# Decay-block copies moved to ScalarE, two multiplies to VectorE and two planner prices raised, in a two-layer decoder trunk

## The chip, the cores and the metric

The kernel runs on one core of one Trainium2 chip. The metric is device time in microseconds (us) for one execution; lower is better. The time of the kernel before is 627.79 us, the median of three runs (627.25, 627.79 and 630.24).

## What is computed

The input is 512 tokens of 1,024 numbers in fp32. Two layers follow one another, each added to its own input. Every multiplication with weights is done as three products of fp32r halves (high part by high part, low by high, high by low).

```python
for layer in range(DEPTH):                     # 2
    h = rms_norm(x, norm_w[layer])
    if layer % 2 == 0:                         # layer 0
        y = even_layer(h, ...)  # projection, mLSTM (4 heads) beside
                                # sparse attention (8 heads), projection
    else:                                      # layer 1
        y = hgrn2_layer(h, ...) # projection, HGRN2 (8 heads), projection
    x = x + y

# mLSTM branch, after its scan h:
h = rms_norm(h, head_norm)
return h * sigmoid(o) * silu(z)

# HGRN2: A holds q.k under the decay between two tokens of a chunk
A = einsum('bhjc,bhsc,bhjsc->bhjs', qj, kj, dec)
o = einsum('bhjs,bhsv->bhjv', A, vj) + einsum('bhjc,bhcv->bhjv', qj*exp(bcum), S)
```

## The kernel before, in words

**The order is planned, not written.** The program's strands call wrapped engines (`Paced`, L540, and `PacedPE`), which only record an operation with its dependencies and a price in nanoseconds from `price` (L516). At the end of each layer `flush` (L391) runs a list scheduler (`schedule`, L283) for 6 rounds, keeps the plan with the earliest end, and only then issues every instruction, from one line, L407. So nearly all rows of the profile have line L407 and are told apart by the names of their tiles, and a changed price redraws the order of all engines and of the DMA queue on SP. On an engine the instructions then run in the planned order.

**Dense products.** `cvt_w` (L736) turns a raw weight tile (`raw`, three buffers, loaded by SP) into a high half `whi` (two copies on ACT) and a low half `wlo` (a subtraction on DVE). The activations are split likewise: `h0h` and `h0l` in layer 0, `h1h` and `h1l` in layer 1, `ymh` and `yml` for layer 0's output projection. PE writes the products to PSUM tiles `mm`, `sc`, `ac`, `mx` and `my`; small products and transposes go to `tp`, `tq` and `sd`.

**Start.** The first products need `whi`, `wlo`, `h0h` and `h0l` for eight pieces of 128 input columns. Beside them ACT squares the input (`acc` and `sq`) for the norm. `rstd` (L892) sums these squares on PE, adds EPS on DVE, takes the power -0.5 on POOL (L900) and spreads the result by PE (`tq<-cs,rs` in layer 1).

**mLSTM tail.** `m_tok(t)` (L1485) divides, norms and gates one chunk of 128 tokens. Its array `nd` is multiplied by `hr` (L1515) and by the gate `gz` (L1517) on POOL, once more on DVE, transposed by PE and split into `ymh` and `yml`. POOL also issues the copies of weight tiles named `wt`.

**HGRN2.** `hgrn(h)` (L1771) builds for a head the array `f` (called `AT` there) of 128 x (4 x 128): its diagonal 32 x 32 blocks come out of `AL` (written by six predicated copies on DVE) by four copies on POOL (L1841 to L1843), each of 32 partitions by 4 x 32; the larger off-diagonal blocks come from `tq` by ACT. Then PE computes `tq<-ivgg,f` and `tq<-Sx,HB`, ACT squares (`hj`), POOL takes a power (`hr`). Transposed keys are evacuated by ACT as `kT`.

Of the kernel before, what the change touches and what calls it, by code (L numbers as in the profile page):

```python
# [16 lines left out]
AF = mybir.ActivationFunctionType  # L17
OP = mybir.AluOpType
# [128 lines left out]
def cust(ap, dims, off=0):  # L147
    return bass.AP(tensor=ap.tensor, offset=ap.offset + off,
                   ap=[list(ap.ap[0])] + [list(d) for d in dims])
# [278 lines left out]
class Mark:  # L428
    t = None
# [86 lines left out]
def price(name, fn, a, k):  # L516

    aps = [x for x in (*a, *k.values()) if isinstance(x, bass.AP)]
    n = max(free_size(x) for x in aps)
    psum = any(x.tensor.name[:3] in PSUMS for x in aps[1:])  # L520
    scal = sum(1 for x in aps[1:] if free_size(x) == 1 and n > 1)
    if name == "A":
        return (55 if psum else 93) + 95 * scal + (88 if "accum_out" in k else 0) + 0.833 * n - (95 if "accum_out" in k else 0)
    if name == "V":
        if fn in ("tensor_scalar", "tensor_copy") and not psum:
            return 67 + 61 * scal + 0.53 * n
        return 67 + 61 * scal + 1.045 * n
    if k.get("op") == OP.pow:
        return 300 + 165 * n
    if fn == "memset":  # L530
        return 32 + 0.86 * n
    if fn == "tensor_copy":
        return 547
    return 150 + (2.1 if fn == "tensor_tensor" else 0.86) * n
# [5 lines left out]
class Paced:  # L540
# [5 lines left out]
    def __getattr__(self, fn):  # L546
        f = getattr(self.eng, fn)

        def go(*a, **k):
            aps = [x for x in a if isinstance(x, bass.AP)]  # L550
            ns = price(self.name, fn, a, k)
            self.flow.work(self.name, ns)
            for x in aps:
                if x.tensor.name in self.flow.last:
                    self.flow.last[x.tensor.name] = self.flow.cur.t
            self.plan.add(self.name, f, a, k, ns)
        return go
# [56 lines left out]
def build(tc, I, out):  # L614
    nc = tc.nc
    fl, pl = Flow(), Plan()
    V, A, P = (Paced(fl, e, n, pl) for e, n in ((nc.vector, "V"), (nc.scalar, "A"), (nc.gpsimd, "P")))
# [3 lines left out]
    with ExitStack() as ctx:  # L621
# [42 lines left out]
        def cut(t, shape, p=slice(0, 128)):  # L664
            n = 1
            for d in shape:
                n *= d
            v = t[p, :n]
            if len(shape) == 1:
                return v  # L670
            ls = "abcdef"[:len(shape)]
            return v.rearrange("p (" + " ".join(ls) + ") -> p " + " ".join(ls), **dict(zip(ls, shape)))
# [32 lines left out]
        hm = cp.tile([128, 16], F32, name="hm")  # L705
# [186 lines left out]
        def rstd(accs, rs, rsB, ev, TPS=TPS, tp_t=tp_t):  # L892
            yield [None, TPS]
            p = tp_t()
            for i in range(NT):
                for a in accs:
                    T.matmul(p[:, i:i + 1], a[:, 128 * i:128 * (i + 1)], shc("one", 1), start=a is accs[0],
                             stop=a is accs[-1], skip_group_check=True)
            V.tensor_scalar(rs, p[:, :4], 1.0 / D, EPS, op0=OP.mult, op1=OP.add)
            P.tensor_tensor(rs, rs, hm[:, :4], op=OP.pow)  # L900
            fl.mark(ev[0]).op = pl.ops[-1]
            yield [None, TPS]
            p = tp_t()
            for i in range(NT):
                T.matmul(p[:, 128 * i:128 * (i + 1)], cust(rs, [[0, 128]], i), idf, start=True, stop=True,
                         skip_group_check=True)
            A.activation(rsB, p, AF.Copy)
            fl.mark(ev[1])
# [36 lines left out]
        with ExitStack() as c0:  # L945
# [45 lines left out]
            rs = rs0  # L991
# [493 lines left out]
            def m_tok(t):  # L1485
                sl = slice(128 * t, 128 * (t + 1))
                yield [E("mh%d" % h) for h in range(4)] + [hb(1)]
                nd = b_t("nd", (4, 129))
                for h in range(4):
                    yield SCS  # L1490
                    p = sc_t()
                    T.matmul(p[:, :129], Sm[0][:, h, sl], vx[0][:, t, h, :], start=True, stop=True,
                             skip_group_check=True)
                    if t:
                        T.matmul(p[:, 256:385], mqk["mq"][:, h, sl], Cx[0][:, t - 1, h, :], start=True, stop=True,
                                 skip_group_check=True)
                        A.activation(nd[:, h, :], p[:, 256:385], AF.Copy,
                                     scale=ex[:, 16 + 4 * t + h:16 + 4 * t + h + 1])
                        V.tensor_tensor(nd[:, h, :], nd[:, h, :], p[:, :129], op=OP.add)
                    else:  # L1500
                        A.activation(nd[:, h, :], p[:, :129], AF.Copy)
                dd = s_t("dd", [128, 4])
                V.scalar_tensor_tensor(dd, nd[:, :, 128], -1.0, nd[:, :, 128], op0=OP.mult, op1=OP.max)
                V.tensor_tensor(dd, dd, ex[:, 32 + 4 * t:36 + 4 * t], op=OP.max)
                rd = s_t("rd", [128, 4])
                V.reciprocal(rd, dd)
                hs = s_t("hs", [128, 4])
                hj = s_t("hj", [128, 128], 1)
                for h in range(4):
                    A.activation(hj, nd[:, h, :128], AF.Square, scale=rd[:, h:h + 1], accum_out=hs[:, h:h + 1])  # L1510
                hr = s_t("hr", [128, 4])
                rsqrt_mean(hr, hs, 4, 1.0 / 128)
                V.tensor_tensor(hr, hr, rd, op=OP.mult)
                n3 = nd[:, :, :128]
                P.tensor_tensor(n3, n3, cust(hr, [[1, 4], [0, 128]]), op=OP.mult)  # L1515
                yield E("go%d" % t)
                P.tensor_tensor(n3, n3, cut(gz[t], (4, 128)), op=OP.mult)  # L1517
                fl.mark(E("mA%d" % t))
                if t == 3:
                    u_end(3)  # L1520
                yield [None, E("gz%d" % t)]
                V.tensor_tensor(n3, n3, cut(gz[t], (4, 128)), op=OP.mult)
                if t == 3:
                    u_end(1)
                yield [None, TPS, has(2) if t == 0 else (lambda: ym)]
                if t == 0:
                    ym["h"], ym["l"] = split("ym")
                tp = tp_t()
                for h in range(4):
                    T.transpose(tp[:, 128 * h:128 * (h + 1)], nd[:, h, :128], idf)  # L1530
                b_end()
                tp4 = cut(tp, (4, 128))
                A.activation(ym["h"][:, :, sl], tp4, AF.Copy)
                V.tensor_tensor(ym["l"][:, :, sl], tp4, ym["h"][:, :, sl].bitcast(F32), op=OP.subtract)
                fl.mark(E("ym%d" % t))

            gz = {}
# [104 lines left out]
            for q in range(4):  # L1642
# [3 lines left out]
                for j in range(2):  # L1646
                    k = 2 * q + j
# [62 lines left out]
        with ExitStack() as c1:  # L1710
# [23 lines left out]
            for j in range(2):  # L1734
                a = s_t(f"AL{j}", [128, 4, 32], 1)
# [35 lines left out]
            def hgrn(h):  # L1771
# [4 lines left out]
                al, AT = AL[h % 2], cut(f, (4, 128))  # L1776
# [3 lines left out]
                for l in range(7):  # L1780
# [14 lines left out]
                    elif l == 5:  # L1795
                        l2 = tq_t()
                        for t in range(8):
                            a, u, b = t // 4, t // 2 % 2, t % 2
# [13 lines left out]
                    else:  # L1812
# [6 lines left out]
                                    op=OP.mult)  # L1819
# [11 lines left out]
                    if l == 4:  # L1831
                        V.copy_predicated(al, cust(cs, [[0, 4], [1, 32]], SC["md"]).bitcast(I32),
                                          cut(lv[:, :256], (4, 64))[:, :, :32])
                        V.copy_predicated(cust(al, [[32, 4], [2, 16]], 1), cust(mh0, [[0, 4], [1, 16]]).bitcast(I32),
                                          cust(lv, [[64, 4], [2, 16]], 33))
                        for l_ in range(1, 5):
                            L = 1 << l_
                            V.copy_predicated(cust(al, [[32, 4], [2 * L, 16 // L], [1, L]], L),
                                              cust(cs, [[0, 4], [L, 16 // L], [1, L]], SC["ml"] + 16 * (l_ - 1)).bitcast(I32),
                                              cust(lv, [[16, 4], [L, 16 // L], [1, L]], 256 + 64 * (l_ - 1)))  # L1840
                        for b in range(4):  # L1841
                            r_ = slice(32 * b, 32 * b + 32)
                            P.tensor_scalar(AT[r_, :, r_], al[r_], 1.0, None, op0=OP.mult)  # L1843
                    yield [m] + ([TQS] if 4 <= l < 6 else [])
                nlv[0] -= 1
                vs = slice(128 * (h % 2), 128 * (h % 2) + 128)
# [17 lines left out]
                op = tq_t()  # L1864
# [11 lines left out]
                hr = s_t("hr1", [128, 4])  # L1876
# [234 lines left out]
```

## Time and profile before

| | before |
|---|---|
| median of three runs | 627.79 us |
| the profiled execution's own time | 629.84 us |
| span of its instructions | 628.1 us |
| PE busy | 613.2 us (98%) |
| DVE busy | 464.9 us (74%) |
| ACT busy | 316.5 us (50%) |
| POOL busy | 129.0 us (21%) |
| bytes moved | 82.90 MB, mean 132 GB/s |
| mean granted clock of PE | 0.995 |

PE is TensorE, DVE is VectorE, ACT is ScalarE, POOL is GpSimd and SP issues most loads. Times of one execution begin at its first instruction. In a timeline row the bracket is the idle time ahead of the instruction and what ended it. A row with "x4" covers four instructions from its start to the end of the last. A PE row's own duration overlaps its neighbours': what counts is from one start to the next.

### The profile page before, as it was taken

The page shows a single profiled execution, that of the slowest core. Times are in us where ns is not written, and L with a number is a line of the kernel's source. Part 1 is how long each engine was busy: PE and PEld are TensorE (multiplying, and loading weights), DVE is VectorE, ACT ScalarE, POOL GpSimd, SP SyncE. Part 2 cuts the span into 40 slices and gives each one's busy share as a digit, 9 for nine tenths or more (in the row PEclk, how much of TensorE's full clock was granted, in tenths as well). Part 3 has the DMA queues.
Part 4 walks back from the last instruction along what each step waited for, and adds up shares of the span by engine and source line. Part 5 has one row for each costly group of instructions (what it writes and reads, how often), then busy time and mean ns, then how long its engine had stood idle before and what let it go on. Part 6 is the DMA issues. An engine that isn't in the chain of part 4 may idle for free.

```text
span 628.1 us, 11709 instructions
## 1 busy us (share of the span) xinstructions
PE 613.2 (98%) x4498; PEld 492.8 (78%) x4498; DVE 464.9 (74%) x977; ACT 316.5 (50%) x746; POOL 129.0 (21%) x174
## 2 busy tenths in 40 slices
PE   7999999999999999999989999998999999999997
PEld 6987787877777777888868877777868877788886
DVE  4879989878978786565555579995579898986441
ACT  6534344666666774473353664553416444546410
POOL 0314442100000010075003110135003230152100
PEclk9999999999999999999999999998999999999999
DMA  8732445624053028059953623563121204474111
GB/s 287 244 145 91 160 147 174 233 103 135 18 148 104 1 56 230 1 157 279 247 171 117 195 72 106 159 205 107 58 79 53 85 2 144 157 291 149 34 68 67
DMA packets 23527, 82.90 MB, mean 132 GB/s; under 512 B 3376, under 2 KB 4272, under 8 KB 20656
## 3 DMA queue, kind: packets, MB, share of 16 engines
q1 hardware_dynamic: 21168, 65.39, 31.8%
q0 software_dynamic: 2304, 16.78, 10.3%
q8 instruction: 35, 0.57, 0.4%
q14 instruction: 20, 0.16, 0.1%
HBM read 77.96 MB, written 20.97 MB: 158 GB/s over the span
## 4 chain that ended last, share of the span: by engine, by line
PE 83%; DVE 8%; DMA 3%; POOL 2%; issue 2%; ACT 1%; SPq 0%; ACTq 0%; DVEq 0%
PE mm L407 28%; PE mx L407 17%; PE my L407 14%; PE sc L407 7%; PE tp L407 5%; PE tq L407 5%; PE ac L407 4%; PE sd L407 2%; DMA raw<-in_wall_dram 2%; DVE wlo L407 2%; DVE x L407 1%; DMA xt<-in_xt_dram 1%; POOL krs L407 1%; DVE q L407 1%; DVE ivgg L407 1%
## 5 line engine op out<-in xcount | busy, mean ns | idle before, releaser
L407 ACT ACTIVATE whi<-raw 128x512 fp32r<-128x512 f32 (+1 forms) x184 | 105.0, 615 | 82.8 <-PE my L407 26.4
L407 DVE TENSOR_TENSOR wlo<-raw,whi 128x1024 fp32r<-128x1024 f32 (+1 forms) x96 | 114.1, 1198 | 24.2 <-ACT whi L407 24.0
L407 PE MATMUL mm<-whi,h0h 128*128 128x512 f32 (+1 forms) x168 | 68.1, 407 | 0.0
L407 PE MATMUL mm<-wlo,h0h 128*128 128x512 f32 (+1 forms) x168 | 67.9, 405 | 0.0
L407 PE MATMUL mm<-whi,h0l 128*128 128x512 f32 (+1 forms) x168 | 67.3, 401 | 0.0
L407 ACT ACTIVATE PP<-sc,nm 128x128 f32<-128x128 f32 (+2 forms) x64 | 33.6, 528 | 29.5 <-DVE nm L407 28.5
L407 DVE CUSTOM_DVE_ANT_0 sc<-sc,cz 128x128 f32<-128x128 f32 (+2 forms) x64 | 31.3, 503 | 14.0 <-PE sc L407 7.9
L407 PE MATMUL mm<-h0h,whi 128*128 128x512 f32 x96 | 39.1, 407 | 0.0
L407 PE MATMUL mm<-h0l,whi 128*128 128x512 f32 x96 | 38.8, 404 | 0.0
L407 PE MATMUL mm<-h0h,wlo 128*128 128x512 f32 x96 | 38.1, 397 | 0.0
L407 DVE TENSOR_TENSOR HB<-HB,tt 128x512 f32<-128x512 f32 x48 | 32.4, 692 | 5.9 <-PE sd L407 3.9
L407 PEld LDWEIGHTS mm<-wlo,h0h 128*128 128x128 f32 x168 | 32.0, 191 | 5.8 <-issue 0.2
L407 PEld LDWEIGHTS mm<-whi,h0h 128*128 128x128 f32 x168 | 31.8, 190 | 5.7 <-DVE sm L407 0.2
L407 PEld LDWEIGHTS mm<-whi,h0l 128*128 128x128 f32 x168 | 31.9, 190 | 5.4
L407 PE MATMUL sc<-kd,q 128*128 128x128 f32 (+3 forms) x128 | 31.4, 331 | 0.0
L407 POOL TENSOR_SCALAR f<-AL 32x128 f32<-32x128 f32 x32 | 22.7, 710 | 37.9 <-DVE AL L407 36.2
L407 ACT ACTIVATE PT<-tp 128x384 f32<-128x384 f32 (+1 forms) x48 | 23.9, 525 | 6.4 <-PE tp L407 6.1
L407 ACT ACTIVATE f<-tq 32x64 f32<-32x64 f32 (+1 forms) x48 | 11.3, 235 | 31.0 <-PE tq L407 30.5
L407 PE MATMUL my<-h1l,whi 128*128 128x512 f32 x64 | 26.3, 411 | 0.0
L407 PE MATMUL mx<-h1l,whi 128*128 128x512 f32 x64 | 26.1, 408 | 0.0
L407 PE MATMUL mx<-h1h,whi 128*128 128x512 f32 x64 | 26.0, 407 | 0.0
L407 PEld LDWEIGHTS sc<-kd,q 128*128 128x128 f32 x128 | 22.7, 191 | 4.1 <-ACT PP L407 0.8
(373 smaller groups left out, 1560.2 us busy)
## 6 DMA issues: line engine op xcount, KB each, us to landing
raw<-in_wall_dram SPq DMA_DIRECT2D x76, 512.0 KB, 4.1
wt<-in_wall_dram POOLq DMA_DIRECT2D x12, 1024.0 KB, 5.5
raw<-wt SPq DMA_DIRECT2D x16, 512.0 KB, 3.5
wt<-wt POOLq DMA_DIRECT2D x4, 1024.0 KB, 11.9
bias<-in_brow_dram SPq DMA_DIRECT2D x9, 256.0 KB, 4.6
xt<-in_xt_dram SPq DMA_DIRECT2D x8, 256.0 KB, 5.8
w<-in_cw_dram SPq DMA_DIRECT2D x2, 1024.0 KB, 9.4
x<-in_xt_dram SPq DMA_DIRECT2D x2, 1024.0 KB, 10.8
```

What stands on the lines that cost most here:

```text
L407: o.fn(*o.a, **k)
```

## The change

The price of an ACT operation rises by 110 ns where its output has fewer than 128 partitions. A price can be given with an operation, and `rstd`'s power gets 1950 ns (the formula gives 300 + 165 x 4 = 960). The last token chunk's two multiplies in `m_tok` go from POOL to DVE. The four diagonal-block copies of each of the eight heads go from POOL to ACT.

```diff
     if name == "A":
-        return (55 if psum else 93) + 95 * scal + ... + 0.833 * n - ...
+        low = 110 if aps[0].ap[0][1] < 128 else 0
+        return low + (55 if psum else 93) + 95 * scal + ... + 0.833 * n - ...
...
-            ns = price(self.name, fn, a, k)
+            ns = k.pop("_price", None) or price(self.name, fn, a, k)
...
-            P.tensor_tensor(rs, rs, hm[:, :4], op=OP.pow)
+            P.tensor_tensor(rs, rs, hm[:, :4], op=OP.pow, _price=1950.0)
...
-                P.tensor_tensor(n3, n3, cust(hr, [[1, 4], [0, 128]]), op=OP.mult)
+                W = V if t == 3 else P
+                W.tensor_tensor(n3, n3, cust(hr, [[1, 4], [0, 128]]), op=OP.mult)
                 yield E("go%d" % t)
-                P.tensor_tensor(n3, n3, cut(gz[t], (4, 128)), op=OP.mult)
+                W.tensor_tensor(n3, n3, cut(gz[t], (4, 128)), op=OP.mult)
...
-                            P.tensor_scalar(AT[r_, :, r_], al[r_], 1.0, None, op0=OP.mult)
+                            A.activation(AT[r_, :, r_], al[r_], AF.Copy)
```

The planner then draws another order. Three places of it follow.

ACT near the start, before; the numbers are the program's buffer numbers (`whi_119` is the high half of the second weight tile, `xt_105` and `xt_108` are the halves of the input):

```order
L407 ACTIVATE whi_119<-raw_106 128x288
L407 ACTIVATE h0h_84<-xt_105,pcs_69 128x512
L407 ACTIVATE acc_90<-xt_105 128x1024
L407 ACTIVATE sq_91<-xt_105 128x1024
L407 ACTIVATE h0h_86<-xt_108,pcs_69 128x512
L407 ACTIVATE whi_119<-raw_106 128x288
L407 ACTIVATE whi_121<-raw_107 128x288 x2
L407 ACTIVATE whi_123<-raw_109 128x288
L407 ACTIVATE sq_91<-xt_108 128x1024
```

The same stretch of ACT in the change:

```order
L407 ACTIVATE whi_119<-raw_106 128x288 x2
L407 ACTIVATE h0h_84<-xt_105,pcs_69 128x512
L407 ACTIVATE h0h_86<-xt_108,pcs_69 128x512
L407 ACTIVATE whi_121<-raw_107 128x288 x2
L407 ACTIVATE acc_90<-xt_105 128x1024
L407 ACTIVATE sq_91<-xt_105 128x1024
L407 ACTIVATE whi_123<-raw_109 128x288
L407 ACTIVATE h0h_86<-xt_108,pcs_69 128x512 x3
L407 ACTIVATE sq_91<-xt_108 128x1024
```

The second half of `whi_119` and both halves of `whi_121` now stand ahead of the two passes over the first input half, `acc_90` and `sq_91`, which stood ahead of them.

ACT in layer 1, around the first two heads' copies, in the change (in the kernel before, the eight copies stand on POOL, and on ACT the `kT` rows stand side by side):

```order
L407 ACTIVATE whi_3629<-raw_3616 128x512 x2
L407 ACTIVATE f_3537<-AL0_3521 32x4x32
L407 ACTIVATE kT_3623<-tq_3622 128x384
L407 ACTIVATE kT_3625<-tq_3624 128x384
L407 ACTIVATE f_3537<-AL0_3521 32x4x32 x3
L407 ACTIVATE f_3553<-AL1_3522 32x4x32 x4
L407 ACTIVATE zz_3613<-ivgg_3561 128x256
L407 ACTIVATE whi_3632<-raw_3631 128x512 x2
```

So on ACT the `kT` evacuations stand behind one of the copies, and `zz` and the next weight tile's halves behind all eight.

PE at the same place in the change, where the first two heads' products read the copied blocks:

```order
L407 MATMUL tq_3637<-ivgg_3561,f_3537 128x128 x2
L407 MATMUL tq_3637<-Sx_3627,HB_3536 128x128
L407 MATMUL tq_3637<-ivgg_3561,f_3537 128x128
L407 MATMUL tq_3637<-Sx_3627,HB_3536 128x128
L407 MATMUL tq_3637<-ivgg_3561,f_3537 128x128
L407 MATMUL tq_3637<-Sx_3627,HB_3536 128x128
L407 MATMUL tq_3643<-ivgg_3561,f_3553 128x128 x2
```

The second head's products (`tq_3643`) now follow the first head's directly; before, six products of 512 columns stood between the two.

## Rows read from the trace of the kernel before

**Rows 1.** The page, part 1: engine, busy us, share of span, instructions.

```profile
PE 613.2 (98%) x4498; PEld 492.8 (78%) x4498; DVE 464.9 (74%) x977; ACT 316.5 (50%) x746; POOL 129.0 (21%) x174
```

**Rows 2.** Waits of PE over the whole span: total us, times, longest us.

```profile
PE sc L407 <- ACT whi L407: 3.3, 3, 1.7
PE tq L407 <- POOL f L407: 1.9, 1, 1.9
PE mm L407 <- ACT ymh L407: 1.4, 1, 1.4
...
PE ac L407 <- POOL hm L407: 1.0, 1, 1.0
...
PE tq L407 <- POOL rs L407: 0.3, 1, 0.3
```

**Rows 3.** Timeline of ACT at the start: start us, us, instruction, bracket.

```profile
10.84 1.05 ACT L407 ACTIVATE acc<-xt 128x1024 f32<-128x1024 f32 x1
11.79 1.04 ACT L407 ACTIVATE sq<-xt 128x1024 f32<-128x1024 f32 x1
...
13.34 1.43 ACT L407 ACTIVATE whi<-raw 128x288 fp32r<-128x288 f32 x4
```

**Rows 4.** Timeline of PE at the start.

```profile
11.79 0.29 PE L407 MATMUL mm<-wlo,h0h 128*128 128x288 f32 x1
13.82 0.53 PE L407 MATMUL sc<-whi,h0h 128*128 128x288 f32 x2 [1.75 <-ACT whi L407]
```

**Rows 5.** Windows: us; PE, PEld, DVE, ACT, POOL busy (instructions); PEclk, DMA share, GB/s.

```profile
15.30:18.70 3.40, 3.40 (x16) 3.40 (x16) 3.40 (x7) 3.40 (x6) 1.39 (x1) 0.50 1.03 397
56.00:98.00 42.00, 41.02 (x209) 33.15 (x207) 38.65 (x84) 16.63 (x40) 17.45 (x20) 1.00 0.53 175
285.00:290.00 5.00, 5.00 (x23) 4.07 (x22) 0.91 (x2) 2.40 (x9) 3.19 (x5) 1.00 1.03 348
...
431.70:435.10 3.40, 3.40 (x13) 2.98 (x13) 1.13 (x4) 1.47 (x8) 1.92 (x4) 0.50 0.38 130
```

**Rows 6.** Timeline of POOL at the first two heads' copies.

```profile
421.63 3.11 POOL L407 TENSOR_SCALAR f<-AL 32x128 f32<-32x128 f32 x4
...
426.80 3.88 POOL L407 TENSOR_SCALAR f<-AL 32x128 f32<-32x128 f32 x4 [1.23 <-DVE AL L407]
```

**Rows 7.** Timeline of PE at the second head's products.

```profile
428.22 0.39 PE L407 MATMUL mx<-h1h,wlo 128*128 128x512 f32 x1
428.45 0.40 PE L407 MATMUL my<-h1h,whi 128*128 128x512 f32 x1
430.74 0.71 PE L407 MATMUL tq<-ivgg,f 128*128 128x128 f32 x4 [1.88 <-POOL f L407]
```

**Rows 8.** Groups by form, whole span: count | busy us, mean ns | idle before, releaser.

```profile
L407 POOL TENSOR_SCALAR f<-AL 32x128 f32<-32x128 f32 x32 | 22.7, 710 | 37.9 <-DVE AL L407 36.2
...
L407 ACT ACTIVATE hj<-tq 128x128 f32<-128x128 f32 x32 | 8.9, 278 | 12.3 <-PE tq L407 11.4
...
L407 ACT ACTIVATE f<-tq 32x64 f32<-32x64 f32 x32 | 6.9, 216 | 24.3 <-PE tq L407 23.9
```

**Rows 9.** Timeline of DVE: a weight subtraction without POOL copies beside it, two with.

```profile
418.34 1.22 DVE L407 TENSOR_TENSOR wlo<-raw,whi 128x1024 fp32r<-128x1024 f32 x1
...
427.26 2.45 DVE L407 TENSOR_TENSOR wlo<-raw,whi 128x1024 fp32r<-128x1024 f32 x2
```

**Rows 10.** Timeline of POOL at the last token chunk's two multiplies.

```profile
288.57 1.04 POOL L407 TENSOR_TENSOR nd<-nd,hr 128x512 f32<-128x512 f32 x1 [0.28 <-DVE hr L407]
289.69 1.20 POOL L407 TENSOR_TENSOR nd<-nd,gz 128x512 f32<-128x512 f32 x1
290.84 0.88 POOL L407 DMA_DIRECT2D wt<-wt  x1
```

**Rows 11.** Timeline of ACT ahead of the output projection's wait.

```profile
315.01 1.15 ACT L407 ACTIVATE whi<-raw 128x512 fp32r<-128x512 f32 x2 [4.43 <-DMA raw<-in_wall_dram]
316.07 0.58 ACT L407 ACTIVATE ymh<-tp 128x512 fp32r<-128x512 f32 x1
```

**Rows 12.** Timeline of PE at the same place.

```profile
316.70 0.50 PE L407 MATMUL mm<-ymh,whi 128*128 128x512 f32 x1 [1.44 <-ACT ymh L407]
317.43 0.50 PE L407 MATMUL mm<-yml,whi 128*128 128x512 f32 x1 [0.23 <-DVE yml L407]
```

**Rows 13.** Timeline of POOL at layer 1's norm.

```profile
361.65 1.95 POOL L407 TENSOR_TENSOR rs<-rs,hm 128x4 f32<-128x4 f32 x1 [8.51 <-DVE rs L407]
```

More of the change, by code (lines that the diff above doesn't have):

```diff
@@ L522, in price @@
     if name == "A":
-        return (55 if psum else 93) + 95 * scal + (88 if "accum_out" in k else 0) + 0.833 * n - (95 if "accum_out" in k else 0)
+        low = 110 if aps[0].ap[0][1] < 128 else 0
+        return low + (55 if psum else 93) + 95 * scal + (88 if "accum_out" in k else 0) + 0.833 * n - (95 if "accum_out" in k else 0)
     if name == "V":
```

## The prediction

> **What bounds the kernel now.** I read the page's busy shares first. PE is busy in 98% of the span, DVE in 74%, ACT in 50%, POOL in 21% [rows 1]. So the time is that of PE, and an edit on another engine counts only where PE waits for that engine. Next comes the list of PE's waits [rows 2], which is short: 3.3 us for `whi` in three pieces (1.7 the longest), 1.9 us in one piece for `f` from POOL, 1.4 for `ymh`, 1.0 for `hm` at the very start, 0.3 for `rs`. Third I went to each of these in the timelines, and fourth I read the granted clock of PE in windows around them. The reader is to see that a wait costs more than its own length: from 15.3 to 18.7 and from 431.7 to 435.1 the clock stands at 0.50 (1.2 GHz, the lower level), while the two windows between them show 1.00 [rows 5]. Both slow stretches come behind the two longest waits, 1.75 us [rows 4] and 1.88 us [rows 7]. At half clock 3.40 us of PE work would have taken 1.70 at full clock, so each stretch costs about 1.7 us. The wait of 1.44 us at 316.70 [rows 12] was not followed by such a stretch.
>
> **The copies.** Per head, four instructions leave POOL and four come to ACT. On POOL the first two heads' copies took 3.11 and 3.88 us; the second four began at 426.80 when `AL` was done, and lasted until 430.68 [rows 6]. PE started a dense product at 428.45, the next start was due 0.23 later (the step from 428.22 to 428.45), and `tq<-ivgg,f` began only at 430.74 [rows 7]: 430.74 - 428.45 - 0.23 = 2.06 us lost, and 1.7 more by the slow clock behind it, 3.7 together. All of it hangs on the copies' duration. On ACT I bound a copy by two groups: `f<-tq`, 32 partitions by 64 elements, 216 ns; `hj<-tq`, 128 by 128 elements, 278 ns; against POOL's mean of 710 [rows 8]. A copy has 32 partitions of 128 elements, so the second has its length; I take 0.28 us, four 1.1 us, between 0.86 (216 ns each) and 1.24 (the planner's 310 ns each). With `AL` ready at 426.7 as before, the second head's copies end near 427.9 and not 430.7, ahead of 428.68, when PE wanted them; the lines of the changed order also put `AL1` earlier on DVE. So the wait goes wholly, **-3.7 us** (ends: -2.1 if the clock falls all the same, 0 if another wait takes its place). The other 24 copies of POOL kept nobody waiting on PE, so they give 0. What comes onto ACT is 32 x 0.28 = 9 us in a layer in which it is half idle. Late next is `zz` and the next weight's two halves, which stand behind the copies: 1.1 us later at the most, with PE having several weights' products in hand.
>
> Should DVE gain from POOL's absence? A weight subtraction took 1.22 us with POOL idle, and two took 2.45 beside the copies, 1.225 each [rows 9]: nothing to gain, so 0. The Trainium skill ("SBUF — State Buffer", section "SBUF: two separate sides") says that a DVE operation with two SBUF inputs and a GpSimd operation that reads SBUF lock each other out for a whole instruction. By that rule each of the two subtractions could lose up to a copy, and moving them would give some tenths more; the trace does not show the loss on DVE's side, and the sum goes by the row.
>
> **The start.** On ACT, `acc` at 10.84 and `sq` at 11.79 ran ahead of the weight halves, which began at 13.34 [rows 3]; PE was through at 11.79 + 0.13 and began again at 13.82, after 1.75 us for `whi` [rows 4]. The changed order puts that half and two more ahead of the squares. They need 0.36 us each (1.43 for four), so the first is done well before 11.79 and PE does not wait for it; the 1.70 of slow clock behind goes too. Against this stands a smaller wait that I expect for `h0l`, which needs DVE and comes one piece at a time; its nearest row is the second wait at the output projection, 0.23 [rows 12], and I take twice that, 0.5. So 1.75 + 1.70 - 0.5 = 3.0 us of lead at 25 us. It does not all arrive: from 56 to 98 DVE is busy for 38.65 of 42 us and PE for 41.02 [rows 5], so PE there is nearly held by DVE, and the 0.98 us that it lacks would grow with the lead if DVE could not start sooner. I let it grow once again, 1.0 us back. Net **-2.0 us** (ends: -3.0, and 0 with all of it lost in that stretch). The squares feed the norm's power later by the three halves, 1.1 us, and PE has dense products in hand until then: 0. The redrawn SP queue also brings two weight tiles ahead of small tables; the tables are wanted much later, 0.
>
> **The power's price.** In layer 1 the power took 1.95 us [rows 13] and PE waited 0.3 for it [rows 2]; priced so, its readers on PE come some products later. **-0.3 us** (ends: 0, -0.5).
>
> **The two multiplies.** They took 1.04 and 1.20 us on POOL and the next thing there was a DMA issue at 290.84 [rows 10]; DVE had 0.91 of 5 us busy [rows 5], so two multiplies of 512 elements fit. PE waits at 316.70 and 317.43, 1.44 and 0.23 us [rows 12], but not for them: ACT stood at a raw weight until 315.01, and `ymh` came behind it at 316.07 [rows 11]. The DMA share was 1.03 from 285 to 290 [rows 5], so a transfer issued 2.2 us sooner mostly displaces others. I take **0** (ends: -1.7, the two waits, if the raw weight lands that much sooner; +0.5 if the earlier transfer delays it).
>
> **The redrawn rest.** Half a dozen other waits of PE, below 1 us each, will be at other places. I take them as equal, 0 (ends: -1, +2).
>
> **Sum.** -3.7 - 2.0 - 0.3 = -6.0 us. The profiled execution took 629.84 with a span of 628.1; it lies 2.05 above the median of 627.79. So 623.8 for a run like it, and 627.79 - 6.0 = **621.8 us** for the median. A measurement of this kernel can tell about 0.5% from no change, 3.1 us: faster is below 624.65, slower above 630.93.
>
> **Rivals.**
> - *The start's lead is lost.* Everything won before 56 us is given back in the stretch that DVE nearly fills [rows 5]; the copies alone count: 627.79 - 4.0 = 623.8. For it: DVE's share there. Against it: nothing in the stretch begins with a load that is late.
> - *Another plan, other waits.* The redrawn order removes two long waits and brings as many at places that I did not follow: 627.8. For it: thousands of instructions move on the strength of prices, and the present waits are all places where a price was wrong. Against it: ACT's new price is nearer to the rows (a copy priced at 93 + 0.833 x 128 + 110 = 310 ns against 278) than POOL's 150 + 0.86 x 128 = 260 against 710 [rows 8].
> - *The change does not do what it says* at the two multiplies is already in the sum, as 0; that it does more there is the case of the raw weight landing sooner: 621.8 - 1.7 = 620.1.
> - *Slower: ACT stands at `AL`.* ACT runs its instructions in order: `ymh` came out only at 316.07, behind weight halves that waited 4.43 us for their load [rows 11]. A copy that waits for `AL` holds `kT`, `zz` and weight halves behind it in the same way, where POOL had little else to do. `AL` was late by 1.23 us at one pair of heads even for POOL [rows 6]. Each time it costs a wait like the present one with its slow clock, 3.7 us. At the first pair it would only replace what is gained; with two more pairs hit, 627.79 + 2 x 3.7 - 2.0 - 0.3 = 632.9. It decides when `AL` comes later than PE's stock of finished weight halves lasts, about 3 us (twelve products of 0.23). Against it: ACT is half idle [rows 1], and the planner knows of the wait. The Trainium skill ("Perfetto Trace Analysis", section "Per-engine timelines") says that ACT, DVE and GpSimd are strict first-in first-out; this trace agrees at 316.07 [rows 11].
>
> **Chances.** The forecast 0.50, of which 0.02 falls into no change; the raw weight sooner 0.04; lead lost 0.17, of which 0.06 is above 624.65, since it lies only 0.9 below the bound; other waits 0.17; slower 0.12. Faster: 0.48 + 0.04 + 0.11 = 0.63. Same: 0.02 + 0.06 + 0.17 = 0.25. Slower: 0.12. The range must leave out at most 0.2. Its low end is 621.8 with the whole lead kept (-1.0), the waits at the output projection gone (-1.7) and a little of the rest (-0.8): 618.3. Its high end takes in the case of other waits and the upper part of the redrawn rest: 627.8 + 1.7 = 629.5. Outside lie the slower case and a tail below. The likeliest case by itself spans 619 to 624.6.
>
> **What would show it.** Right: no wait of PE for `f`, and no window at 0.50 near 430; no wait of 1.7 us for `whi` near 13, and full clock from 15 to 19; a copy on ACT of 0.22 to 0.31 us; the wait for `ymh` still there. Wrong: PE waits for `f` from ACT, or for `kT` or `whi` behind it, in layer 1; or PE's idle between 56 and 98 grown from 1 to 4 us; or new waits over 1 us at places not named here.

## The result, and the profile after

The changed kernel took 621.10 us (median of six runs, 619.22 to 622.40) against 628.13 for the kernel before (six runs, 627.25 to 630.24) on the same chip: ratio 0.9884, 95% interval 0.9862 to 0.9906. The forecast was 621.8 us and faster. The profiled execution took 622.05 us.

The busy shares of the page after, to be read against [rows 1]; PE's busy time fell by 2.7 us with the same 4498 matmuls, and the 22.7 us of copies left POOL:

```profile
span 620.3 us, 11687 instructions
...
PE 610.5 (98%) x4498; PEld 492.5 (79%) x4498; DVE 464.6 (75%) x979; ACT 326.6 (53%) x778; POOL 106.0 (17%) x140
```

PE's waits after, to be read against [rows 2]. `f` from POOL and `rs` are gone from the list, `whi` has shrunk from 3.3 us to 0.6, `ymh` stands where it stood, and the wait for `kd` has grown from 0.5 us to 1.2. Not all of what `whi` lost is the change's: a second profile of the same program has 2.1 us for it (1.45 at 6.25 and 0.69 at 8.79), and what is gone from both is the wait of 1.75 us at 13.82 [rows 4].

```profile
PE tp L407 <- DVE kd L407: 1.2, 1, 1.2
PE mm L407 <- ACT ymh L407: 1.2, 1, 1.2
...
PE sc L407 <- ACT whi L407: 0.6, 1, 0.6
PE mm L407 <- DVE wlo L407: 0.4, 1, 0.4
```

ACT at the start, after, where [rows 3] has the squares at 10.84 and the weight halves at 13.34; now the four halves at 9.39 and 11.51 run before the squares:

```profile
9.39 0.78 ACT L407 ACTIVATE whi<-raw 128x288 fp32r<-128x288 f32 x2 [0.31 <-DMA raw<-in_wall_dram]
10.07 1.40 ACT L407 ACTIVATE h0h<-xt,pcs 128x512 fp32r<-128x512 f32 x2
11.51 0.78 ACT L407 ACTIVATE whi<-raw 128x288 fp32r<-128x288 f32 x2
12.19 1.04 ACT L407 ACTIVATE acc<-xt 128x1024 f32<-128x1024 f32 x1
13.14 1.04 ACT L407 ACTIVATE sq<-xt 128x1024 f32<-128x1024 f32 x1
```

Windows after (columns as in [rows 5]). Both places that stood at clock 0.50 are at 1.00. But another window of 3.40 us, from 51.7, now reads 0.56:

```profile
431.70:435.10 3.40, 3.40 (x20) 2.86 (x19) 2.33 (x6) 1.37 (x2) 0.00 (x0) 1.00 0.00 0
15.30:18.70 3.40, 3.40 (x28) 3.40 (x27) 3.40 (x6) 3.40 (x7) 0.00 (x0) 1.00 1.03 393
51.70:55.10 3.40, 3.40 (x12) 2.63 (x11) 3.13 (x5) 0.00 (x0) 0.15 (x1) 0.56 0.28 60
```

The copies on ACT, after. The seven that run in a row took 2.23 us and were done at 424.40:

```profile
420.94 0.31 ACT L407 ACTIVATE f<-AL 32x128 f32<-32x128 f32 x1 [0.19 <-DVE AL L407]
421.27 0.87 ACT L407 ACTIVATE kT<-tq 128x384 f32<-128x384 f32 x2
422.17 2.23 ACT L407 ACTIVATE f<-AL 32x128 f32<-32x128 f32 x7
```

PE at the same place, after: the second head's products start at 426.89 without a bracket, where [rows 7] has 430.74 and 1.88 us of idle time:

```profile
425.26 0.68 PE L407 MATMUL tq<-ivgg,f 128*128 128x128 f32 x4 [0.24 <-DVE Sx L407]
...
426.89 0.61 PE L407 MATMUL tq<-ivgg,f 128*128 128x128 f32 x4
```

Two landmarks say how much had arrived by when. The output projection of layer 0 begins at 315.84 after and at 316.70 before [rows 12], 0.86 us earlier; the spans end 7.8 us apart. So in these two executions most of the gain came in layer 1. That this is partly an accident of where the slow stretches fell is what the experiments show.

### The profile page after: what moved, and what is told of

Read it like the earlier page. It is cut to its first block, busy times and chain, and to the rows that moved or that the text cites. A ratio compares the mean times of both kernels' runs of the same rounds, so it can differ in the third digit from the quotient of the medians.

```text
span 620.3 us, 11687 instructions
## 1 busy us (share of the span) xinstructions
PE 610.5 (98%) x4498; PEld 492.5 (79%) x4498; DVE 464.6 (75%) x979; ACT 326.6 (53%) x778; POOL 106.0 (17%) x140
## 4 chain that ended last, share of the span: by engine, by line
PE 86%; DVE 6%; DMA 3%; issue 1%; POOL 1%; ACT 1%; SPq 0%; ACTq 0%; DVEq 0%
PE mm L407 30%; PE mx L407 17%; PE my L407 15%; PE sc L407 7%; PE tp L407 5%; PE tq L407 5%; PE ac L407 4%; DMA raw<-in_wall_dram 3%; PE sd L407 2%; DVE wlo L407 1%; POOL krs L407 1%; DVE q L407 1%; DVE x L407 1%; DVE HB L407 1%; DVE ivgg L407 1%
## 5 line engine op out<-in xcount | busy, mean ns | idle before, releaser
L407 POOL TENSOR_TENSOR ivgg<-ivgg,zz 128x256 f32<-128x256 f32 x16 | 17.7, 1106 | 66.0 <-ACT zz L407 66.0
L407 PE MATMUL tp<-cs,PP 128*128 128x128 f32 x160 | 26.7, 276 | 0.0
```

Of the source, the lines that this page charges most:

```text
L407: o.fn(*o.a, **k)
```

## The experiments

Every variant is planned anew by the same planner, except where the text says that the plan is kept. Ratios are to the kernel before on the same chip.

**Each part by itself.** The four parts of the change, one at a time.

```diff
-                            P.tensor_scalar(AT[r_, :, r_], al[r_], 1.0, None, op0=OP.mult)
+                            A.activation(AT[r_, :, r_], al[r_], AF.Copy)
```

> Only the diagonal-block copies go to ScalarE; layer 0's order is that of before. My theory: the wait of 2.06 us on PE for f and the 1.7 us of slow clock behind it go, so 3.7 us less than before (ratio 0.994), while the wait for whi near 13.8 and its slow clock stay. Rival (the gain of layer 1 comes from the redrawn order that the two prices bring): within 1 us of before. Rival (ScalarE stands at AL with weight halves behind it): no faster, with waits of PE for whi, kT or f in layer 1.

Measured: 626.53 against 628.79 us, ratio 0.9970 (0.9951 to 0.9989). Half of the 3.7 us. The wait for `f` is gone; `whi` still costs PE 3.4 us at the start.

```diff
-            P.tensor_tensor(rs, rs, hm[:, :4], op=OP.pow)
+            P.tensor_tensor(rs, rs, hm[:, :4], op=OP.pow, _price=1950.0)
```

> Only the norm's power is priced 1950 ns. My theory: the changed order on ScalarE at the start comes from this price alone; PE is about 2.9 us ahead at 50 us, as in the changed kernel, most of it given back before 100 us, and the 0.3 us wait for rs goes: 1 to 1.5 us less than before (ratio 0.998), the 430 us wait stays. Rival (all lead is lost): 628, ratio 1.000. Rival (the whole lead arrives where no slow clock comes at 52 us): 625, ratio 0.995.

Measured: 624.28 against 628.79 us, ratio 0.9931 (0.9911 to 0.9951): 4.3 us by the ratio, three times what I expected and the largest of the four. It draws the start's new order by itself. The wait for `f` is still there:

```profile
427.07 0.71 PE L407 MATMUL tq<-ivgg,f 128*128 128x128 f32 x4 [1.90 <-POOL f L407]
```

No stretch of slow clock followed that wait of 1.90 us:

```profile
430.00:434.00 4.00, 4.00 (x22) 3.26 (x21) 2.16 (x7) 1.23 (x5) 1.20 (x2) 1.00 0.01 2
```

```diff
-        return (55 if psum else 93) + ...
+        low = 110 if aps[0].ap[0][1] < 128 else 0
+        return low + (55 if psum else 93) + ...
```

> Only the ACT price of outputs under 128 partitions rises by 110 ns; the order changes in both layers, no work moves. My theory: it changes which small waits there are and nothing else, 628 plus or minus 1.5 us. Rival (the unexplained waits in the sd groups near 466 and 470, 1.4 us, went by this price): 626.5 or less, with those waits gone.

Measured: 628.55 us, ratio 0.9996 (0.9976 to 1.0016): nothing, as expected. The unexplained waits in `sd` fell from 1.4 to 0.6 us in its profile and the time did not follow.

```diff
-                P.tensor_tensor(n3, n3, cust(hr, [[1, 4], [0, 128]]), op=OP.mult)
+                W = V if t == 3 else P
+                W.tensor_tensor(n3, n3, cust(hr, [[1, 4], [0, 128]]), op=OP.mult)
...
-                P.tensor_tensor(n3, n3, cut(gz[t], (4, 128)), op=OP.mult)
+                W.tensor_tensor(n3, n3, cut(gz[t], (4, 128)), op=OP.mult)
```

> Only the last token chunk's two multiplies go to VectorE; hardly any other instruction moves. My theory: 0, the time of before within 0.5 us, the wait for ymh near 316.7 stays within 0.3 us of 1.44. Rival (the wt transfer is issued 2 us sooner and the raw weight that ScalarE stands at lands sooner): 1.2 to 1.7 us less and the ymh wait gone.

Measured: 628.81 us, ratio 1.0003 (0.9984 to 1.0023): nothing. POOL issues the `wt` transfer at 288.52, where it stood at 290.84 [rows 10], but the one behind it waits 7.98 us for a transfer and goes out at 297.41, where before it went at 297.00, and PE's wait for `ymh` is 1.46 us:

```profile
288.52 0.90 POOL L407 DMA_DIRECT2D wt<-wt  x1
297.41 0.82 POOL L407 DMA_DIRECT2D wt<-wt  x1 [7.98 <-DMA wt<-wt]
```

```profile
316.97 0.50 PE L407 MATMUL mm<-ymh,whi 128*128 128x512 f32 x1 [1.46 <-ACT ymh L407]
```

Beside the one near 15, this profile has its slow stretch behind that wait, and none behind a wait of 2.0 us for `f` at 432.46, the reverse of the kernel before [rows 5]:

```profile
318.30:321.70 3.40, 3.40 (x10) 2.69 (x9) 1.61 (x2) 0.00 (x0) 0.00 (x0) 0.54 0.55 159
431.70:435.10 3.40, 2.64 (x19) 2.46 (x20) 0.85 (x3) 1.10 (x5) 3.09 (x6) 1.00 0.80 267
```

**Engine, order or price.** Three kernels take the copies apart. In the first the plan and the order are the changed kernel's, and only the engine that does the copies is put back.

```diff
-                            A.activation(AT[r_, :, r_], al[r_], AF.Copy)
+                            A.activation(AT[r_, :, r_], al[r_], AF.Copy,
+                                         _emit=lambda o, i, _: nc.gpsimd.tensor_scalar(o, i, 1.0, None, op0=OP.mult))
```

> The plan is the changed kernel's, with its prices and its order, but the 32 diagonal-block copies are issued on GpSimd at the places where the plan has them on ScalarE. Theory A (the engine counts: a copy takes 0.5 to 1.5 us on GpSimd and 0.31 on ScalarE): PE waits for f again at the first pair of heads, 0.5 to 2 us, so 1 to 3 us more than the changed kernel, ratio 0.990 to 0.994. Rival B (the order counts, not the engine): as the changed kernel, 0.9884 within 0.002, with no wait for f over 0.3 us.

Measured: 623.07 against 628.91 us, ratio 0.9928 (0.9903 to 0.9952). The ratio is as theory A has it, but the mechanism is not: PE's list has no wait for `f`. The eight copies (L1847 is the line that issues them here) took 5.28 us and ended at 425.09, 0.6 us before PE began the second head's products:

```profile
419.81 5.28 POOL L1847 TENSOR_SCALAR f<-AL 32x128 f32<-32x128 f32 x8 [1.77 <-DVE AL L407]
```

```profile
425.70 0.61 PE L407 MATMUL tq<-ivgg,f 128*128 128x128 f32 x4
```

Its interval touches that of the changed kernel, so whether the engine is worth a microsecond in that order stays open. One wait of PE is there, 0.44 us for `yo` at 430.87, that the changed kernel's second profile, in the same order, does not have; what it hangs on was not followed.

In the second the copies stay on POOL and get a price near what they take.

```diff
-                            P.tensor_scalar(AT[r_, :, r_], al[r_], 1.0, None, op0=OP.mult)
+                            P.tensor_scalar(AT[r_, :, r_], al[r_], 1.0, None, op0=OP.mult, _price=780.0)
```

> The copies stay on GpSimd and are priced 780 ns instead of 260; PE's, ACT's and SP's orders stay those of before, DVE writes AL somewhat earlier. Theory A (the engine counts): the copies still end some 2 us late, the wait for f shrinks by no more than a third, ratio 0.999 to 1.000. Rival C (a wrong price was the cause, and the planner mends it where the copies are): the wait for f goes, ratio 0.997 as with the copies alone on ScalarE.

Measured: 625.88 against 628.91 us, ratio 0.9961 (0.9942 to 0.9980). Theory A falls. PE's order is that of before; DVE writes `AL` ahead of `Sx` and the weight subtraction, and POOL begins at 424.65, where [rows 6] has 426.80:

```profile
424.65 3.13 POOL L407 TENSOR_SCALAR f<-AL 32x128 f32<-32x128 f32 x4 [0.50 <-DVE AL L407]
```

It ends at 427.78, and PE waits 0.33 us in place of 1.88. Not all of that is the earlier start. PE itself was 1.34 us earlier in this execution (its last product ahead of the wait began at 427.11, in [rows 7] at 428.45), so against PE the copies began 0.8 us sooner; and they took 3.13 us in place of 3.88. The two make up the 1.55 us, about half each:

```profile
427.11 0.40 PE L407 MATMUL my<-h1h,whi 128*128 128x512 f32 x1
427.83 0.71 PE L407 MATMUL tq<-ivgg,f 128*128 128x128 f32 x4 [0.33 <-POOL f L407]
```

In the third the plan is that of before, and only the engine changes.

```diff
-                            P.tensor_scalar(AT[r_, :, r_], al[r_], 1.0, None, op0=OP.mult)
+                            P.tensor_scalar(AT[r_, :, r_], al[r_], 1.0, None, op0=OP.mult,
+                                            _emit=lambda o, i, *_, **__: nc.scalar.activation(o, i, AF.Copy))
```

> The plan is that of before, unchanged in order; the copies are issued on ScalarE at the places where the plan has them on GpSimd. Theory A: the wait of 1.9 us for f goes, ratio 0.996 to 0.998 as with the copies alone. Rival D (ScalarE stands at AL, whi and zz behind it): PE waits for whi or kT of 1 us or more in layer 1, ratio 0.999 or above.

Measured: 625.59 against 628.91 us, ratio 0.9956 (0.9940 to 0.9972). The second head's four copies take 1.25 us and end at 427.71, PE begins without a wait:

```profile
426.46 1.25 ACT L1845 ACTIVATE f<-AL 32x128 f32<-32x128 f32 x4
```

```profile
427.85 0.65 PE L407 MATMUL tq<-ivgg,f 128*128 128x128 f32 x4
```

PE's order is the same in both kernels, so the two profiles can be set side by side, product by product: PE is 0.5 us ahead of before at 418 us and 4.2 ahead at 437, so 3.7 us were won here, the predicted term. The medians, over executions with and without a slow stretch at this place, give 2.8.

So two cures work on one wait: a quicker engine in the old order (0.9956), or an honest price on the old engine (0.9961). They are not told apart by the times.

**Where the price of the power works.** The price in layer 0's plan alone:

```diff
-            P.tensor_tensor(rs, rs, hm[:, :4], op=OP.pow)
+            P.tensor_tensor(rs, rs, hm[:, :4], op=OP.pow, _price=960.0 if tp_t is tq_t else 1950.0)
```

> The power is priced 1950 ns in layer 0 alone and 960 in layer 1. My theory: the start's order on ScalarE comes from layer 0's price, so nearly all of the 4.3 us of the price stays: ratio 0.993 to 0.995; the wait for rs near 360 is back, 0.3 to 0.5 us. Rival: half or more of the gain was layer 1's price: ratio 0.997 or above.

Measured: 625.13 against 628.91 us, ratio 0.9955 (0.9939 to 0.9970), just outside the narrow range that I gave; 2.8 us of the 4.3 are layer 0's. The two ratios' intervals overlap, so the share of layer 1 is not sharp.

Then another price, 1100 ns in both layers:

```diff
-            P.tensor_tensor(rs, rs, hm[:, :4], op=OP.pow)
+            P.tensor_tensor(rs, rs, hm[:, :4], op=OP.pow, _price=1100.0)
```

> Only the power's price, and 1100 ns in place of 960 or 1950, near the 1.06 us that it took in layer 0 of before; another order results, with both halves of the second weight tile ahead of the squares on ScalarE and those of the third behind. Theory A (the order of these squares and weight halves is what counts, whatever price draws it): half or more of the start's gain, 1.3 us or more, ratio 0.994 to 0.998. Rival (a price near the truth gives the whole gain): ratio 0.9931 or below. Rival (1950 was a lucky draw): ratio 0.999 to 1.003.

Measured: 629.35 against 628.01 us, ratio 1.0021 (1.0005 to 1.0036). The rival of the lucky draw holds. And this is the run that says most: its start is as good as the changed kernel's. PE's last product of 288 columns began at 24.18 before, at 21.92 after, and here at 21.41. The row before, the row after, and the row here:

```profile
24.18 0.29 PE L407 MATMUL mm<-wlo,h0h 128*128 128x288 f32 x1
```

```profile
21.92 0.30 PE L407 MATMUL mm<-wlo,h0h 128*128 128x288 f32 x1
```

```profile
21.41 0.29 PE L407 MATMUL mm<-wlo,h0h 128*128 128x288 f32 x1
```

That lead of 2.8 us was lost, and 1.05 us more, before the output projection, which began at 317.75 (316.70 before, [rows 12]). Set side by side with before, at points where PE had done the same products, PE was 2.2 us ahead at 26.8, still 1.8 ahead at 59.4, and 1.1 behind at 97.8 (times of before). So most went between 59 and 98 us, and PE's waits between 56 and 99 show 2.2 us of it: they are 3.1 us here, against 0.9 before. Here:

```profile
62.94 0.63 PE L407 MATMUL tp<-cs,x 128*128 128x128 f32 x4 [1.19 <-DVE q L407]
...
78.61 0.41 PE L407 MATMUL tp<-cs,ce 128*128 128x128 f32 x2 [0.52 <-DVE q L407]
...
97.28 0.63 PE L407 MATMUL tp<-cs,x 128*128 128x128 f32 x4 [0.90 <-DVE csm L407]
...
98.89 0.30 PE L407 MATMUL tp<-cs,ce 128*128 128x128 f32 x1 [0.52 <-DVE kd L407]
```

Before:

```profile
69.23 0.66 PE L407 MATMUL tp<-cs,x 128*128 128x128 f32 x4 [0.38 <-DVE x L407]
...
97.82 0.41 PE L407 MATMUL tp<-cs,ce 128*128 128x128 f32 x2 [0.53 <-DVE kd L407]
```

**The changed kernel again, and two without the ACT price.**

> The changed kernel once more, on the chip of the next three. Expected 0.9884 within 0.002 of before, 621 to 622 us; the place and number of slow-clock stretches differ from profile to profile.

Measured: 621.61 against 628.01 us, ratio 0.9898 (0.9882 to 0.9915). This profile has no slow stretch at 15, 52 or 432. The three waits of PE between 56 and 98 us:

```profile
75.50 0.30 PE L407 MATMUL tp<-cs,ce 128*128 128x128 f32 x1 [0.42 <-DVE q L407]
...
92.77 0.50 PE L407 MATMUL mm<-h0h,wlo 128*128 128x512 f32 x1 [0.40 <-DVE wlo L407]
...
94.71 0.63 PE L407 MATMUL tp<-cs,x 128*128 128x128 f32 x4 [1.21 <-DVE kd L407]
```

and the window that was slow in the first profile:

```profile
51.70:55.10 3.40, 3.40 (x17) 2.59 (x16) 3.40 (x5) 1.98 (x5) 0.74 (x2) 1.00 0.46 114
```

The output projection starts at 314.04 here, 2.66 us ahead of before:

```profile
314.04 0.49 PE L407 MATMUL mm<-ymh,whi 128*128 128x512 f32 x1 [1.23 <-ACT ymh L407]
```

Next, the ACT price in layer 1's plan only:

```diff
-        low = 110 if aps[0].ap[0][1] < 128 else 0
+        low = 110 if LOW[0] and aps[0].ap[0][1] < 128 else 0
...
+            LOW[0] = True
             pl.flush(ROUNDS, ...)
```

> The changed kernel, with the 110 ns on ScalarE's small outputs only in layer 1's plan; layer 0's order is then the one that the power's price alone draws. Theory: the 110 ns in layer 0 are what brings the 1.2 us wait for kd and the 0.4 us wait for wlo at 94 to 97 us, so 1.5 to 2 us less than the changed kernel: ratio 0.985 to 0.987 to before. Rival (the lead is lost in VectorE's stretch whatever the order): as the changed kernel, 0.9884 within 0.002, with PE's waits between 56 and 98 us as long.

Measured: 620.87 us, ratio 0.9880 (0.9859 to 0.9902). The waits for `kd` and `wlo` are gone from the list and one of 0.7 us for `csm` came; the time is not told apart from the changed kernel's, so the gain that I expected isn't shown. Last, none of the ACT price:

```diff
-        low = 110 if aps[0].ap[0][1] < 128 else 0
-        return low + (55 if psum else 93) + ...
+        return (55 if psum else 93) + ...
```

> The changed kernel without the 110 ns at all: power's price, copies on ScalarE, multiplies on VectorE. If the parts add (0.9931 and 0.997): 0.990. Theory: layer 0 as good as with the power's price alone, layer 1 worse than the changed kernel's: 0.988 to 0.991. Rival (the ACT price is needed so that the copies go in time): a wait for f or for whi behind the copies of 1 us or more, ratio 0.992 or above.

Measured: 620.08 us, ratio 0.9881 (0.9862 to 0.9901), the same as the changed kernel. The ACT price isn't needed. No version here is shown to beat the changed kernel.

## Why the prediction was right, and where not

The time, its sign and its size were right, but part of that is luck: two terms were off in opposite directions. The parts, one by one:

- **The copies, -3.7 us.** The wait went wholly, as said. As a mean over executions the term was too large: 1.9 us by `copies_alone`, 2.8 in the old order. The step that failed is "each stretch costs about 1.7 us" counted in full behind this wait. Of the fourteen profiles six have a wait of 1.9 to 2.6 us for `f`, and four of these six have a slow stretch between 425 and 440; of the eight without the wait none has one. So the wait does bring the slow stretch, but not each time. A copy took 307 ns (mean of 32), not 280. And "all of it hangs on the copies' duration" was wrong: in `pool_copies_priced_780` about half of what the wait lost came from beginning the copies sooner.
- **The start, -2.0 us.** PE's lead when the start was over was 24.18 - 21.92 = 2.3 us in the first profile and 2.9 in the second (its last such product began at 21.28), for 3.0 predicted; the waits that stayed are for `whi` (0.6 us in the first profile, 2.1 in the second, all before 9 us), not for `h0l`. The 1.0 us given back in VectorE's stretch is what the second profile shows: 2.03 us of waits there against 0.91. That the lead arrived as 0.86 in the first profile and 2.66 in the second is mostly the slow stretch near 52: side by side with before, the lead in the first profile fell there from 2.6 us (at 42.0) to 0.8 (at 55.6). Over all profiles the output projection of layer 0 starts at 315.47 to 317.54 in the six with the start's old order and at 313.27 to 315.84 in the seven with the power priced 1950 in layer 0, 2.3 us apart in the mean; by the medians layer 0's price is worth 2.8 us. So the lead does arrive, and -2.0 was near it. The step "the 1.70 of slow clock behind goes too" is not shown: of six profiles with the start's old order two have the stretch at 15, three have it at 49 to 53, and one has none.
- **Why it arrives.** I explained the arrival by the lead. `power_price_1100` had the lead, kept 1.8 us of it to 59.4 us and lost all of that in VectorE's stretch, my rival "the start's lead is lost". The gain thus needs the order that 1950 ns happened to draw there too; which of its instructions counts was not tried.
- **The power, -0.3 us.** PE's wait for `rs` is gone (`tq<-cs,rs` without a bracket, though the power took 1.96 us as before). With what else that price moved in layer 1 it comes to 1.5 us, by the difference of two ratios whose intervals overlap.
- **The multiplies, 0,** and **no change of speed for DVE, 0:** right; the `wt` issue came 2.3 us sooner and the next one 0.4 us later.
- **The redrawn rest, 0.** The unexplained waits ("issue") fell by 1.5 us between the two profiles, but they come to 1.1 us in the changed kernel's second profile and to between 0.5 and 1.7 in the other kernels, in either order, so I don't count them as an effect of the change. One of my signs of being wrong did show, a new wait over 1 us: 1.21 us for `kd` at 96.59, inside the stretch where I let 1.0 us go back.
- **ACT standing at `AL`,** the slower rival: ACT did stand there, 1.7 us in three pieces, and PE did not wait for anything behind it.

```profile
ACT f L407 <- DVE AL L407: 1.7, 3, 1.3
```

By the runs the sum reads: the power's price -4.3, the copies -1.9 to -2.8, the other two 0; the changed kernel measured -6.4 to -7.3. The total of -6.0 was met with the copies too large and the power's price too small (-2.0 and -0.3 against -4.3, most of the difference in layer 1, whose 1.5 us was not explained beyond the 0.3); that the two errors nearly cancel is luck.

## What to carry to other kernels

Where a planner sets the order, a wait for a slow engine may be a wrong price: try the honest price in place before work is moved, and read what the plan then does earlier. An early lead is worth only what the next stretch that another engine nearly fills lets through, so look at that stretch's waits and not at the start alone. A changed price redraws far more than the place it was meant for; measure each part alone, and a second value of the price, before a gain is put down to its being right.

## What the runs showed of the hardware

**Slow stretches come and go.** Every stretch that I looked at is about 3.4 us at 1.2 GHz. The same program has it in one execution and not in the next: the changed kernel at 51.7 in one profile and not in the other, with PE busy in that window in both. The times follow: of six runs of the changed kernel three with a mean granted clock of 1.000 took 619.22 to 620.97 us, and three at 0.997 took 621.22 to 622.40. The means of the two groups are 1.5 us apart, about half of the whole spread.

**Half the pace at the start, with the clock reading 1.00.** In the first profile of the changed kernel PE's products of 288 columns came 0.24 us apart up to 10.0 us and 0.13 apart from 10.4 on; before they came 0.13 apart from 6.05 on. The clock of the window from 6 to 8 us reads 1.00 in both.

```profile
6.42 0.44 PE L407 MATMUL ac<-whi,h0h 128*128 128x288 f32 x1
6.66 0.44 PE L407 MATMUL mm<-whi,h0h 128*128 128x288 f32 x1
```

`power_price_alone` and `power_price_1100` show the same up to 9.2 and 9.3 us, the changed kernel's second profile does not. Thirteen such products cost 1.4 us more (13 x 0.11), so leads at the start are to be compared with this in mind. PE also came to the next weight half later, which fits that the first profile lacks the wait of 0.69 us that the second has at 8.79. What brings the half pace is not shown.

**VectorE and GpSimd get in each other's way.** In the profile after, `krs<-kss` of 128x4 took 1.24 us beside a weight subtraction on DVE (89.11 to 90.34) and 0.19 at 95.02:

```profile
89.15 1.24 POOL L407 TENSOR_SCALAR krs<-kss 128x4 f32<-128x4 f32 x1 [6.25 <-DVE kss L407]
...
92.76 0.75 POOL L407 TENSOR_TENSOR qk<-qk,knB 128x256 f32<-128x256 f32 x1
...
95.02 0.19 POOL L407 TENSOR_SCALAR krs<-kss 128x4 f32<-128x4 f32 x1 [1.51 <-DVE kss L407]
```

and a subtraction that began beside `qk` took 1.78 us, where [rows 9] has 1.22:

```profile
92.82 1.78 DVE L407 TENSOR_TENSOR wlo<-raw,whi 128x1024 fp32r<-128x1024 f32 x1
```

I had read [rows 9] as no loss on DVE. It is so for those copies, and these rows show that it isn't so everywhere: each engine was held for most of the other's instruction (POOL for 1.05 us of 1.23, DVE for 0.56 of 0.75), which is the rule of the Trainium skill ("SBUF — State Buffer", section "SBUF: two separate sides") that the prediction set aside. It fits the copies of before as well: in the chain of waits the three that PE waited for took 1.48, 1.17 and 0.54 us, and the first two lay beside the two subtractions of [rows 9]. Moving a copy out of that pairing was not tried alone.

```profile
427.38 1.48 POOL f L407
...
428.93 1.17 POOL f L407
...
430.15 0.54 POOL f L407
```
